# A fused transformer block on one core: attention's turns and values at other distances behind the logits, a compression layer cut in two jobs, later keys in other tiles

## The chip, the cores and the metric

The kernel runs on one core of a Trainium2 chip. The metric is the device time of the whole program in microseconds (us). Before the change it was 1020.26 us as the median of 3 runs (1019.53 to 1020.44). Differences of over about 0.2% (2 us) can be told from no change.

## The reference, cut to what matters

For 512 tokens of 1024 features the reference computes a half-weighted SwiGLU layer, a mixer, a second SwiGLU layer and a norm, in fp32:

```python
x = x + 0.5 * swiglu(rmsnorm(x, norm_ffn1), w_ffn1_gate, w_ffn1_up, w_ffn1_down)
x = x + hybrid_mixer(rmsnorm(x, norm_mix), ...)      # the change is in here
x = x + 0.5 * swiglu(rmsnorm(x, norm_ffn2), w_ffn2_gate, w_ffn2_up, w_ffn2_down)
return rmsnorm(x, norm_final)
```

The mixer projects the tokens to queries, keys and values for 16 heads of 64 features. Eight are MoBA heads (0 to 7): with 512 tokens and blocks of 256 their selection takes in all earlier blocks, so they come to causal attention with a bias by distance. Eight are NSA heads (8 to 15, in two groups of four): each is the gated sum of three attentions, over selected keys (`ks`), over a window (`kw`) and over 31 compressed keys (`cmp`). The compressed keys and values come out of a small two-layer network over blocks of 32 tokens, silu(blocks @ w1) @ w2, one for keys and one for values. All heads are put side by side and multiplied by `w_out`.

## The kernel before, in words

**Exact products.** TensorE multiplies in a reduced fp32 form, so an operand is split into a high and a low half (ScalarE copies, VectorE or GpSimd subtracts) and `mm3` (L86) makes three products: L87, L88, L89. Weights come in chunks of 128 x 1024 through three `raw` tiles; `halves` (L73) splits them (`whi` on ScalarE L81, `wlo` L82). While `side[0]` is set, from L1062 to the end of the mixer, `wlo` is made by GpSimd, otherwise by VectorE.

**Attention in steps.** A head, or a head and kind for NSA, is three steps of `chunks_of_head` (L878), over the four blocks of 128 queries: (0, 1), (2), (3). A step has three parts. *Logits* (L886): products L908 and L909 into a PSUM tile `ps_s`; VectorE adds the bias and takes the row's extreme (L916), ScalarE takes the exponential (L918, Exp), and where the step ends a row's work VectorE inverts the sum (L923) and GpSimd scales the row in place (L929) by it and by a gate. The rows lie in `lpn` tiles (four of them) and `lp` tiles (two). *Turn* (L931): TensorE transposes the scaled blocks (L938) into `ps_t`, ScalarE copies the high half to `th` (L941), VectorE makes the low half `tl` (L942). A head's first turn, of block column 0, needs the scaled rows of all four query blocks. *Values* (L947): products L93 and L94 of `th` and `tl` with the values into a PSUM tile `po`. After a head's last values `out_halves` (L850) splits the head's output into `oT`. Between NSA heads stand four steps of `cmp_pair` (L963): their logits go to `ps_c`, their turn writes a `th` tile of which there is one, shared with the 512-wide turns, and their values (L1006) read it. There are 76 steps, 52 of NSA and 24 of MoBA.

**The order on TensorE** is written out by hand (L1093 on). In round i the logits of step i are issued, then the turn of step i-4, then the values of step i-7; after each, `run` (L1034) issues other work, in units of three products (0.69 us), up to a target which a table `share` sets. The other work is a `stream` (L824) of jobs, each loading its weights two jobs ahead: `pre`, which is done before the first step, `fill` and `last` (L1021 to L1031). `proj` (L580) are the projections (eight units, PSUM `pp`), `w_out` (L805) is the output projection (PSUM `pw`), `khid` and `vhid` are the first layer of the compression for keys and values (PSUM `pc`), and `ksec` and `vsec` its second layer: `second` (L749) transposes the hidden values (L753, PSUM `pct`), splits them (L758, L759), loads and splits w2 (L761 to L765) and multiplies (PSUM `pck`) in one job. `need` (L1052) runs the stream until something is there. The order on the other engines is set by the tile scheduler, from the order of the program and its own estimate of when things are ready; tiles are given out of pools by it too. PSUM tags s, t, o and mm have two banks each; `pc`, `pct`, `pck`, `ps_t` share t, and `ps_c`, `pp`, `pw` share mm.

**Keys and queries** of MoBA: `moba_t` (L650) scales a projection; `stack_k` (L620) splits it and moves the halves by eight DMAs on SyncE's queue (L609) into four tiles, two of the high halves first; `stack_q` (L611) does so with four DMAs into two `aq` tiles. The keys of all four pairs go to `ak` tiles, six in all, which compression uses too. The keys of pairs 0 and 1 are stacked as soon as they are projected, those of pairs 2 and 3 by `moba_split` (L660), which `ahead` (L1040) calls when head 3 or 5 starts. NSA's values and keys lie in 12 `kvn` tiles, which the outputs `oT` of heads 0 to 7 take over.

## Time and profile before

One execution was profiled. Its span is from the first to the last instruction; its own time has some 2 us around that.

| | us |
|---|---|
| median of the runs | 1020.26 |
| the profiled execution | 1019.0 |
| its span | 1017.2 |
| TensorE busy in it | 982.8 |
| VectorE busy | 716.8 |
| ScalarE busy | 511.9 |
| GpSimd busy | 153.2 |

The attention stage runs from 424.7 us (the first logits) to 639 us (the last values). TensorE's idle time and its granted clock there are what to look for: a row of the waits names who waited, for whom, how long in all, how often and the longest. A row of the timeline has start, duration, engine, line, operation, tile written <- tiles read, and in brackets the idle time ahead of it with what ended it. PE is TensorE, DVE VectorE, ACT ScalarE, POOL GpSimd, SP SyncE.

### The profile page before, as it was taken

Reading aid. Unit: us, or ns where it says so; the run is one execution under the profiler, and the core shown is the slowest. Engines: PE = TensorE matmul, PEld = TensorE weight load, DVE = VectorE, ACT = ScalarE, POOL = GpSimd, SP = SyncE. Lnnn points to the kernel's source line nnn. Section 1 sums busy time; section 2 is a strip of 40 time slices with the busy share of each in tenths; the row PEclk is TensorE's granted clock in tenths of the full one; section 3 lists DMA queues with packets and bytes.
Section 4 is the critical chain, followed back from the end, with each engine's and each line's share of the span. In section 5 each row is a group of like instructions: output and inputs, shape, how many; then the busy total and the mean of one; then the engine's idle time right before and its main releaser. Section 6 shows DMA issues by size and latency. Waiting matters only on the chain. (4 is left out here: it accounts for less than half of the span.)

```text
span 1017.2 us, 15533 instructions
## 1 busy us (share of the span) xinstructions
PE 982.8 (97%) x5944; PEld 866.3 (85%) x5944; DVE 716.8 (70%) x1117; ACT 511.9 (50%) x871; POOL 153.2 (15%) x187
## 2 busy tenths in 40 slices
PE   9999999999999999879899997999999999999997
PEld 7889899999999898668778786888899999999995
DVE  5995686777774666557887766678957777767743
ACT  7553443444443554656766756545534444444444
POOL 0000000000000343235444542610000000000002
PEclk9999999999999999979999999999999999999999
DMA  9534265332301236721232522363332323432102
GB/s 331 215 103 132 76 209 146 125 108 80 116 34 39 78 108 200 223 67 52 61 81 73 153 84 55 110 232 107 101 125 92 116 79 109 125 113 92 45 1 83
DMA packets 45742, 113.86 MB, mean 112 GB/s; under 512 B 10049, under 2 KB 14866, under 8 KB 45668
## 3 DMA queue, kind: packets, MB, share of 16 engines
q1 hardware_dynamic: 45380, 112.73, 35.0%
q8 instruction: 47, 0.77, 0.3%
q14 instruction: 27, 0.22, 0.1%
q10 hardware_dynamic: 288, 0.14, 0.1%
HBM read 100.08 MB, written 5.30 MB: 104 GB/s over the span
## 5 line engine op out<-in xcount | busy, mean ns | idle before, releaser
L197 ACT ACTIVATE sph<-aw 128x1024 fp32r<-128x1024 f32 x114 | 121.0, 1061 | 238.5 <-PE pu L88 118.5
L198 DVE TENSOR_TENSOR spl<-aw,sph 128x1024 fp32r<-128x1024 f32 x114 | 139.3, 1222 | 37.0 <-ACT sph L197 36.9
L81 ACT ACTIVATE whi<-raw 128x1024 fp32r<-128x1024 f32 (+3 forms) x115 | 111.9, 976 | 103.9 <-PE pd L88 30.9
L88 PE MATMUL pd<-h,whi 128*128 128x512 f32 x320 | 126.4, 395 | 0.0
L87 PE MATMUL pd<-h,whi 128*128 128x512 f32 x320 | 126.1, 394 | 0.0
L89 PE MATMUL pd<-h,wlo 128*128 128x512 f32 x320 | 125.2, 391 | 0.0
L82 DVE TENSOR_TENSOR wlo<-raw,whi 128x1024 fp32r<-128x1024 f32 (+3 forms) x89 | 110.2, 1240 | 20.4 <-ACT whi L81 18.9
L89 PE MATMUL pu<-th,spl 128*128 128x256 f32 x384 | 106.9, 278 | 0.0
L87 PE MATMUL pu<-th,sph 128*128 128x256 f32 x384 | 106.9, 278 | 0.0
L88 PE MATMUL pu<-tl,sph 128*128 128x256 f32 x384 | 106.7, 278 | 0.0
L287 DVE TENSOR_TENSOR aw<-aw 128x1024 f32<-128x1024 f32 x64 | 78.0, 1220 | 29.1 <-DMA aw<-in_wgu 29.1
L469 DVE SCALAR_TENSOR_TENSOR x<-pd,x 128x512 f32<-128x512 f32 x72 | 49.3, 688 | 46.9 <-PE pd L89 46.9
L88 PEld LDWEIGHTS pu<-tl,sph 128*128 128x128 f32 x384 | 72.6, 189 | 3.9
L87 PEld LDWEIGHTS pu<-th,sph 128*128 128x128 f32 x384 | 72.1, 188 | 4.3
L87 PE MATMUL pgu<-xo,whi 128*128 128x512 f32 x192 | 75.1, 391 | 0.2 <-ACT xo L123 0.2
L88 PE MATMUL pgu<-xo,whi 128*128 128x512 f32 x192 | 74.8, 390 | 0.3 <-DVE xo L124 0.3
L89 PE MATMUL pgu<-xo,wlo 128*128 128x512 f32 x192 | 74.8, 389 | 0.0
L89 PEld LDWEIGHTS pu<-th,spl 128*128 128x128 f32 x384 | 72.1, 188 | 0.0
L89 PEld LDWEIGHTS pd<-h,wlo 128*128 128x128 f32 x320 | 60.1, 188 | 13.4
L89 PE MATMUL pw<-xo,spl 128*128 128x256 f32 x256 | 70.9, 277 | 0.0
L87 PE MATMUL pw<-xo,sph 128*128 128x256 f32 x256 | 70.8, 276 | 0.0
L88 PE MATMUL pw<-xo,sph 128*128 128x256 f32 x256 | 70.8, 276 | 0.0
(254 smaller groups left out, 2465.2 us busy)
## 6 DMA issues: line engine op xcount, KB each, us to landing
aw<-in_wgu SPq DMA_DIRECT2D x64, 512.0 KB, 4.0
raw<-in_wgu SPq DMA_DIRECT2D x23, 512.0 KB, 5.6
raw<-in_wd SPq DMA_DIRECT2D x22, 512.0 KB, 3.5
raw<-in_wd2a SPq DMA_DIRECT2D x18, 512.0 KB, 3.6
raw<-in_w_a SPq DMA_DIRECT2D x16, 512.0 KB, 3.5
raw<-in_w SPq DMA_DIRECT2D x8, 512.0 KB, 5.0
aq<-xo SPq DMA_DIRECT2D x32, 128.0 KB, 2.3
raw<-in_w_o SPq DMA_DIRECT2D x16, 256.0 KB, 2.7
```

The lines of the kernel that those rows point to most:

```text
L81: nc.scalar.activation(hi[:, s], src[:, s], AF.Copy)
L82: (nc.gpsimd if side[0] else nc.vector).tensor_tensor(lo[:, s], src[:, s], f32(hi[:, s]), ALU.subtract)
L87: nc.tensor.matmul(p, w[0], v[0], start=first, stop=False, skip_group_check=again)
L88: nc.tensor.matmul(p, w[0], v[1], start=False, stop=False, skip_group_check=again)
L89: nc.tensor.matmul(p, w[1], v[0], start=False, stop=last, skip_group_check=again)
L197: nc.scalar.activation(hi, v, AF.Copy)
L198: nc.vector.tensor_tensor(lo, v, f32(hi), ALU.subtract)
L287: nc.vector.tensor_tensor(to, x, y, op)
L469: nc.vector.scalar_tensor_tensor(xs[d], p, 0.5, xs[d], ALU.mult, ALU.add)
```

## The change

The turn of a step now stands six steps behind its logits (four before) and the values nine (seven before). In each round the values come first, then the turn, then the logits. The first six rounds get 1.5 units of other work more, the other shares are a little lower, and a fifth `lpn` tile is added. `second` is cut into two jobs, `turned` (transposes and their halves) and `second` (the products), with other jobs between; w2 is now loaded and split while the third chunk of the first layer is multiplied. In `pre`, `vhid`'s chunks stand ahead of the last chunk of `vm` (MoBA's values). Only the keys of pair 0 are stacked at once; those of pairs 1 and 3 go to `kvn` tiles, those of pairs 0 and 2 to `ak` tiles.

```diff
-                if kind == "k" and pair < 2:
+                if kind == "k" and not pair:
                     moba_k(pair)
...
-            got["k", pair] = stack_k(got["k", pair], [akt() for _ in range(4)])
+            got["k", pair] = stack_k(got["k", pair], [kvn() if pair % 2 else akt() for _ in range(4)])
...
-            if pair >= 2:
+            if pair:
                 moba_k(pair)
...
+                    if c == 8:
+                        second_weights()
...
-            def second(w):
+            def second_weights():
+                w2 = tmp.tile([128, 2, 64], F32, name="w2", tag="t", bufs=6)
+                nc.sync.dma_start(w2, A["w2"][which])
...
+            def turned(w):
                 hid = p[1]
                 pp = pt("t", "pct")
...
+            def second(w):
+                w2h, w2l, hh, hl = kept
                 pp = pt("t", "pck")
...
-            return proj(8 + which, blocks), [hidden(c) for c in range(0, 16, 4)], (None, second)
+            return proj(8 + which, blocks), [hidden(c) for c in range(0, 16, 4)], [(None, turned), (None, second)]
...
-                    lp = ap.tile([128, 384], F32, name="lpn", tag="lpn", bufs=4)
+                    lp = ap.tile([128, 384], F32, name="lpn", tag="lpn", bufs=5)
...
-               proj(11, nsa_k("kw")), khid[3], vm[2], ksec, vhid[0], proj(12, nsa_q(0)), vhid[1], vm[3], vhid[2], vhid[3],
-               (None, marked)]
-        fill = [proj(13, nsa_q(1)), vsec, proj(14, nsa_q(2)), proj(15, nsa_q(3))]
+               proj(11, nsa_k("kw")), khid[3], vm[2], ksec[0], vhid[0], vhid[1], proj(12, nsa_q(0)), ksec[1],
+               vhid[2], vhid[3], vm[3], (None, marked)]
+        fill = [proj(13, nsa_q(1)), vsec[0], proj(14, nsa_q(2)), vsec[1], proj(15, nsa_q(3))]
...
-        share = [0.65 if i < n_nsa else 0.6 for i in range(len(steps) + 7)]
+        share = [0.6 if i < n_nsa else 0.55 for i in range(len(steps) + 9)]
...
+            if i < 6:
+                share[i] += 1.5
...
-            for i in range(len(steps) + 7):
-                for j, lag in enumerate((0, 4, 7)):
+            for i in range(len(steps) + 9):
+                for n, (j, lag) in enumerate(((2, 9), (1, 6), (0, 0))):
                     if 0 <= i - lag < len(steps):
                         steps[i - lag][j]()
```

TensorE has 5748 rows of instructions before and after; only their order differs. Three places, each with TensorE's or ScalarE's rows (the changed kernel has other line numbers there: L919 and L920 are the logits, L949 the turn, L929 the exponential, L747 the Silu, L758 w2h).

TensorE before, ahead of the first turn (`ps_t`), at the end of the fifth logits (`ps_s`):

```order
L87 MATMUL pp<-xo,whi 128x512
L88 MATMUL pp<-xo,whi 128x512
L89 MATMUL pp<-xo,wlo 128x512
L908 MATMUL ps_s<-kvn,aq 128x384
L909 MATMUL ps_s<-kvn,aq 128x384
L938 MATMUL ps_t<-ident,lpn 128x128 x3
L938 MATMUL ps_t<-ident,lp 128x128
```

The same place now, at the end of the sixth logits:

```order
L87 MATMUL pp<-xo,whi 128x512
L88 MATMUL pp<-xo,whi 128x512
L89 MATMUL pp<-xo,wlo 128x512
L919 MATMUL ps_s<-kvn,aq 128x512
L920 MATMUL ps_s<-kvn,aq 128x512
L87 MATMUL pp<-xo,whi 128x512
L88 MATMUL pp<-xo,whi 128x512
L89 MATMUL pp<-xo,wlo 128x512
L949 MATMUL ps_t<-ident,lpn 128x128 x3
L949 MATMUL ps_t<-ident,lp 128x128
```

Between the first logits and the first turn stood five logits and 6 products of a projection; now there are six logits, 30 products and two small transposes.

ScalarE before, from the last chunk of `vm` to the first exponentials (`hid` is the hidden layer of the compressed values, L745 its Silu):

```order
L690 ACTIVATE vm<-pv,rc_94 128x8x64 x4
L81 ACTIVATE whi<-raw 128x1024 x2
L743 ACTIVATE hid<-pc 64x256
L81 ACTIVATE whi<-raw 128x1024
L918 ACT_TABLE_LOAD
L918 ACTIVATE lpn,m<-lpn,m 128x128
L918 ACTIVATE lpn,m<-lpn,m 128x256
L918 ACTIVATE lpn,m<-lpn,m 128x384
L745 ACT_TABLE_LOAD
L745 ACTIVATE hid<-hid 64x256
L918 ACT_TABLE_LOAD
L918 ACTIVATE lp,m<-lp,m 128x512
```

The same place now:

```order
L81 ACTIVATE whi<-raw 128x1024
L758 ACTIVATE w2h<-w_4117 128x128
L747 ACTIVATE hid<-hid 64x256
L690 ACTIVATE vm<-pv,rc_94 128x8x64 x4
L81 ACTIVATE whi<-raw 128x1024
L929 ACT_TABLE_LOAD
L929 ACTIVATE lpn,m<-lpn,m 128x128
L929 ACTIVATE lpn,m<-lpn,m 128x256
L929 ACTIVATE lpn,m<-lpn,m 128x384
L929 ACTIVATE lp,m<-lp,m 128x512
```

The Silu (now L747) stands ahead of `vm`, and one table load is left where there were three.

TensorE before, at the second layer for the values:

```order
L93 MATMUL po<-th,kvn 128x128
L94 MATMUL po<-tl,kvn 128x128
L753 MATMUL pct<-ident,hid 128x64 x2
L87 MATMUL pck<-w2h,hh 32x64
L88 MATMUL pck<-w2l,hh 32x64
L89 MATMUL pck<-w2h,hl 32x64
```

And now, at its transposes:

```order
L89 MATMUL pp<-xo,wlo 128x512
L766 MATMUL pct<-ident,hid 128x64 x2
L919 MATMUL ps_s<-kvn,aq 128x384
L920 MATMUL ps_s<-kvn,aq 128x384
L87 MATMUL pp<-xo,whi 128x512
```

The products into `pck` followed the transposes at once; now 47 rows stand between, some 10 us of TensorE's work.

## The prediction

> **What bounds the kernel now.** I read the page first, then the busy time by stage, then TensorE's waits by stage, then the timeline at the longest of them.

> ```profile
> span 1017.2 us, 15533 instructions
> PE 982.8 (97%) x5944; PEld 866.3 (85%) x5944; DVE 716.8 (70%) x1117; ACT 511.9 (50%) x871; POOL 153.2 (15%) x187
> ```

> TensorE (PE) is busy for 97% of the span, so it is the bound, and its work is the same after the change: 5748 rows in another order. What can be won is its idle time, 1017.2 - 982.8 = 34.4 us, and time in which it runs at a lower clock. The next view has engines by stretch; PEclk is the granted clock.

> ```profile
> core 0: us, PE busy (x) PEld busy (x) DVE busy (x) ACT busy (x) POOL busy (x), PEclk, DMA share, GB/s
> 434.00:441.00 7.00, 6.14 (x24) 5.10 (x24) 2.75 (x10) 4.43 (x15) 3.30 (x6) 0.57 0.11 30
> 451.00:457.00 6.00, 5.17 (x26) 4.66 (x27) 2.70 (x11) 1.76 (x6) 0.00 (x0) 0.50 0.61 176
> 460.00:600.00 140.00, 131.00 (x752) 110.42 (x751) 110.69 (x304) 96.18 (x243) 71.13 (x94) 1.00 0.31 84
> 613.00:618.00 5.00, 4.77 (x24) 4.33 (x24) 2.36 (x8) 3.19 (x9) 0.00 (x0) 0.66 0.45 118
> ```

> Two short stretches behind 434 and 451 us, and one behind 613, have a clock near half. Now TensorE's waits from 400 to 460 us (the second compression layers and the start of attention):

> ```profile
> PE ps_t L938 <- POOL lpn L929: 2.7, 3, 2.2
> PE pck L87 <- ACT w2h L764: 2.7, 2, 1.8
> PE ps_t L938 <- POOL lp L929: 2.4, 1, 2.4
> PE pck L88 <- DVE w2l L765: 2.0, 1, 2.0
> ```

> From 460 to 600 us (the rest of NSA and the first MoBA heads):

> ```profile
> PE ps_t L938 <- DVE tl L942: 3.6, 4, 1.5
> PE po L94 <- DVE tl L942: 1.3, 3, 0.5
> PE ps_s L909 <- DMA ak<-xo: 1.2, 1, 1.2
> PE po L93 <- ACT th L941: 1.0, 2, 0.5
> PE ps_t L938 <- DVE m L923: 0.8, 1, 0.8
> PE ps_s L908 <- DVE m L916: 0.6, 2, 0.3
> PE ps_t L938 <- POOL lp L929: 0.5, 2, 0.2
> ```

> From 600 to 660 us (the last MoBA heads):

> ```profile
> PE ps_s L909 <- DMA ak<-xo: 2.3, 1, 2.3
> PE ps_t L938 <- DVE tl L942: 1.4, 2, 0.9
> PE ps_t L938 <- POOL lp L929: 1.4, 2, 1.0
> PE ps_s L908 <- DMA ak<-xo: 1.3, 1, 1.3
> ```

> These sum to 9.8, 9.0 and 6.4: 25.2 of the 34.4 us of idle time are in the stage that the change reorders. So the question for each row is whether the new order puts work into it.

> **The first turn.**

> ```profile
> 424.69 0.22 PE L908 MATMUL ps_s<-kvn,aq 128*128 128x128 f32 x1
> 430.93 0.33 PE L938 MATMUL ps_t<-ident,lpn 128*128 128x128 f32 x1 [2.20 <-POOL lpn L929]
> 434.86 0.47 PE L938 MATMUL ps_t<-ident,lp 128*128 128x128 f32 x1 [2.43 <-POOL lp L929]
> 435.56 0.63 PE L88 MATMUL pp<-xo,whi 128*128 128x512 f32 x1
> 435.99 0.63 PE L89 MATMUL pp<-xo,wlo 128*128 128x512 f32 x1
> 445.28 0.39 PE L87 MATMUL pp<-xo,whi 128*128 128x512 f32 x1
> 445.51 0.39 PE L88 MATMUL pp<-xo,whi 128*128 128x512 f32 x1
> ```

> The turn's last block comes 434.86 - 424.69 = 10.2 us after the first logits. ScalarE has a detour within that:

> ```profile
> 429.91 1.28 ACT L745 ACT_TABLE_LOAD   x1
> 431.20 0.42 ACT L745 ACTIVATE hid<-hid 64x256 f32<-64x256 f32 x1
> 432.93 0.72 ACT L918 ACTIVATE lp<-lp,m 128x512 f32<-128x512 f32 x1
> ```

> A load, the Silu and a load back take 432.93 - 429.91 = 3.0 us. The new order does the Silu ahead of `vm`, so the chain is some 10.2 - 3.0 = 7.2 us. TensorE's side: products of 512 columns start every 445.51 - 445.28 = 0.23 us, so the 30 products that now stand ahead of the first turn are 6.9 us; six logits are some 2.4 us (the five of before took 424.69 to 428.7, less 6 products at 0.23 and 0.5 of waits, 2.1 us). The turn is due after 9.3 us, against a chain of 7.2. This wait, 2.7 + 2.4 = 5.1 us, goes. What is late next: behind the first turn the six steps issued ahead come due on VectorE and ScalarE together, with the halves of two projections among them. I trace the halves of the first turn and the rows of the fourth step to within a microsecond of their use, and leave 2.0 us of new waits: the term is **3.1** (0 to 5.1).

> **The second layers.** The rows of `pck` are 2.7 + 2.0 = 4.7 us, 0.9 of it in the keys' job and 3.8 in the values'. Now w2 is loaded and split under the first layer, and some 7 us (a projection and two `pc` chunks) and 10 us of other products lie between the transposes and `pck`. What stands in front of `hh` and `hl` on ScalarE and VectorE can't be ten times their 0.3 us. I leave 0.2: **4.5**.

> **The clock.** At full clock products start every 0.23 us, in the stretch behind the first turn every 435.99 - 435.56 = 0.43. The windows give a clock of 0.57 and 0.50: of the 6.1 us from 434.86 and the 5.2 us from 451.8, 0.43 and 0.50 are lost, 2.6 + 2.6 = **5.2**. Each stretch stands right behind two idle times of some 2 us, and the 140 us from 460 have the full clock, so it goes with those waits. [...]

> **NSA's other waits**, 460 to 600 us without the DMA's 1.2: 3.6 + 1.3 + 1.0 + 0.8 + 0.6 + 0.5 = 7.8 us. Rows that wait for the scaled rows (0.8 and 0.5) go: the distance from a head's last logits to its first turn was 2.9 to 6.3 us of TensorE's work in NSA and is now 5.2 to 8.7. The others:

> ```profile
> 470.64 0.50 PE L94 MATMUL po<-tl,kvn 128*128 128x512 f32 x1 [0.50 <-DVE tl L942]
> 501.12 0.52 PE L938 MATMUL ps_t<-ident,lpn 128*128 128x128 f32 x3 [1.37 <-DVE tl L942]
> ```

> The first stands behind the values of compression: the next 512-wide turn can only be copied when those have read the one `th` tile, and its values follow 1.5 us later in both orders. I halve it (1.3 + 1.0 gives 1.1), since the turn's copy now stands ahead of the exponentials on ScalarE. The second is a bank of `ps_t`: the `tl` that frees it is queued on VectorE behind a logits row that TensorE has not made yet. Turns follow each other as closely as before, but there are fewer such inversions in VectorE's order (7 for 11 over all steps), so I take half of 3.6, 1.8. The 0.6 stays. Sum: 1.3 + 1.1 + 1.8 = **4.2** (0 to 7.8).

> Against it stands what the change makes shorter: the values now follow their turn by 3.4 to 8.3 us of TensorE's work in NSA, where it was 4.8 to 8.3. The copy and its low half need some 0.6 + 0.7 us, more when exponentials stand ahead. No row of before shows this wait apart from the places above. If one in four of 48 turns is late by 0.25 us, that is **-3.0** (0 to -10).

> **The keys.** Pair 2's wait (1.2, at head 4) goes: the `ak` tiles hold only two pairs now, and on SyncE its eight DMAs stand a head earlier: **1.2**. Pair 3's (2.3 + 1.3) stays nearly:

> ```profile
> 607.67 4.95 SPq L609 DMA_DIRECT2D ak<-xo  x8
> 610.60 0.30 PE L908 MATMUL ps_s<-ak,aq 128*128 128x128 f32 x1 [1.28 <-DMA ak<-xo]
> 613.23 0.30 PE L909 MATMUL ps_s<-ak,aq 128*128 128x128 f32 x1 [2.33 <-DMA ak<-xo]
> ```

> Its keys are projected at the last moment in both orders, and what it waits for is eight issues of 0.62 us in a row, not a tile. The logits of head 6 now stand 3.7 us behind the projection instead of 3.1: **0.4** (counting the jitter of one DMA). The clock behind 613 us stays low.

> **The last heads and the end.** There the steps have no other work between them. The waits for `lp` (1.4) go with the longer distance, those for `tl` (1.4) stay: **1.4** (0 to 2.8). At the end one wait is new:

> ```profile
> 639.15 0.28 PE L94 MATMUL po<-tl,vm 128*128 128x128 f32 x1
> 642.01 1.26 DVE L867 TENSOR_TENSOR kvn<-to,u 64x512 fp32r<-64x512 f32 x1 [0.41 <-ACT u L866]
> ```

> From the last values to the output's low half are 643.27 - 639.15 = 4.1 us. Eight units (5.5 us) covered them; five units (3.4 us) are left, since the values come two rounds later: **-0.5**.

> **The sum**: 3.1 + 4.5 + 5.2 + 4.2 - 3.0 + 1.2 + 0.4 + 1.4 - 0.5 = 16.5 us. Against the profiled execution, 1019.0 (span 1017.2): 1002.5. The median of the runs shown is 1.3 above it, so the median to expect is 1020.3 - 16.5 = 1003.8 us.

> **Rivals.** (1) *The start stays a chain.* On ScalarE a split of weights (`whi`) whose load is issued late stands ahead of the first exponential; if that load lands some 3 us late, the first turn is late again and the clock falls behind it. Then 3.1 and one 2.6 are gone: a gain of 10.8, 1009.5 us. For it: the rows of `whi` are where ScalarE can be held; against it: the chain has 2.1 us to spare. (2) *The clock stays low where it was*, because it comes of something else than the waits: without 5.2 the gain is 11.3, 1009.0 us. [...] Against it: the full clock from 460 to 600 us, with shorter waits in the same kind of work. (3) *Slower: the halves of the turns become the bound.* VectorE is busy for 110.7 of 140 us from 460 to 600, ScalarE for 96.2, both in strict order; the values stand up to some 3 us closer to their turn, 2.5 us behind it in the last heads. If each of the 72 turns' halves comes late to its values, the loss reaches the other terms' 19.5 us at 0.27 us a turn; at 0.35 it is 25 us, and the time 1020.3 - 19.5 + 25 = 1026 us. For it: waits for `tl` and `th` are the most of NSA's. Against it: they stand at a shared tile and a bank, not at the ordinary turns. (4) *The keys' new tiles are not free in time*, since `kvn` tiles are freed only by the last values of NSA's first group: the waits of head 2 or 6 grow to some 4 us more; a gain of 12, 1008 us. Against it: the DMAs of pair 1 stand on SyncE's queue two heads ahead of their use.

> **How the numbers follow.** The forecast holds for gains from 13 to 24 us: 0.63. Rival 1 has 0.16, rival 2 0.07, rival 4 0.05. Rival 3 has 0.05, and 0.04 is a milder form of it, 0.20 to 0.27 us a turn: gains of 5 to 0 us, half of them under 2. Differences of over 0.2% (2.0 us) can be told from no change; so faster by more has 0.93, no change 0.02, slower 0.05. The range: its low end takes the terms of the start, of NSA and of the last heads near their upper bounds, 16.5 + 1 + 3 + 2 = 22.5 and a little, 997 us; its high end takes in rivals 1, 2 and 4, 1011.5 us.

> **What would show it.** Right: no wait of over 1 us for L929's rows ahead of the first turn; one table load between `vm` and the first exponentials; no wait at `pck`; a granted clock of 1.00 from 424 to 460 us; one DMA wait left, at head 6, of 3 to 3.6 us. Wrong: a wait of 2 us or more ahead of any of the first six turns, or waits at `po` that sum to over 6 us. A TensorE idle time of under 15 us in all would mean that I gave the values too much.

## The result, and the profile after

The changed kernel took 1006.98 us as the median of 4 runs (1002.16 to 1008.83), the kernel before 1020.17 on the same chip (1019.53 to 1020.44): a ratio of 0.9858, 95% interval 0.9827 to 0.9888, 13.2 us faster. The forecast was 1003.8 in a range from 997 to 1011.5. The profiled execution was the fastest of the four, 1002.16 us with a span of 1000.4: against the profiled execution of before (1019.0) it is 16.8 us faster, where the working came to 16.5.

The page of the changed kernel, its first lines:

```profile
span 1000.4 us, 15514 instructions
PE 974.6 (97%) x5944; PEld 860.0 (86%) x5944; DVE 719.5 (72%) x1117; ACT 509.4 (51%) x869; POOL 154.9 (15%) x187
```

TensorE's idle time fell from 34.4 to 1000.4 - 974.6 = 25.8 us, by 8.6. The other 8.2 us are busy time, 982.8 to 974.6, for the same 5944 instructions. Most of that is the clock: in the profile of before, three stretches at half clock (433.18 to 440.01, 450.24 to 457.07 and 614.08 to 617.49 us) hold 5.15, 5.24 and 3.41 us of busy time at a granted clock of 0.50, so by an estimate half of it, 6.9 us, is lost. Where the other 1.3 us lie is open. The busy time by stretch, with the same columns as before:

```profile
424.00:434.00 10.00, 8.66 (x43) 6.88 (x42) 7.78 (x21) 7.85 (x17) 5.95 (x7) 1.00 0.58 195
434.00:441.00 7.00, 7.00 (x41) 5.91 (x40) 5.37 (x19) 5.68 (x18) 5.00 (x6) 1.00 0.56 134
451.00:457.00 6.00, 6.00 (x40) 5.27 (x39) 4.20 (x16) 3.80 (x11) 3.57 (x7) 1.00 0.47 143
460.00:600.00 140.00, 127.37 (x728) 106.68 (x727) 111.33 (x298) 94.71 (x237) 70.05 (x93) 1.00 0.35 90
```

The clock is 1.00 in the two stretches that had 0.57 and 0.50, and the trace has no low stretch ahead of the end of the program. At the start, TensorE's first logits and first turn:

```profile
425.95 0.33 PE L919 MATMUL ps_s<-kvn,aq 128*128 128x128 f32 x1 [1.34 <-DVE vm L691]
435.92 0.49 PE L949 MATMUL ps_t<-ident,lpn 128*128 128x128 f32 x3
436.25 0.27 PE L949 MATMUL ps_t<-ident,lp 128*128 128x128 f32 x1
```

The turn waits for nothing. TensorE's waits from 400 to 460 us:

```profile
PE ps_s L919 <- DVE vm L691: 1.3, 1, 1.3
PE ps_t L949 <- DVE vc L799: 0.6, 1, 0.6
```

From 460 to 600 us:

```profile
PE ps_t L949 <- DVE tl L953: 4.7, 7, 1.1
PE ps_s L920 <- DMA kvn<-xo: 2.5, 1, 2.5
PE pw L88 <- DVE o L878: 1.7, 1, 1.7
PE ps_t L949 <- DVE m L934: 1.7, 1, 1.7
PE pw L87 <- ACT o L874: 0.7, 1, 0.7
PE po L94 <- DVE tl L953: 0.5, 1, 0.5
PE ps_t L949 <- DVE mc L997: 0.3, 1, 0.3
PE ps_s L919 <- DMA kvn<-xo: 0.2, 1, 0.2
PE ps_s L919 <- DVE m L927: 0.2, 1, 0.2
```

From 600 to 660 us one row is left:

```profile
PE ps_t L949 <- DVE tl L953: 2.3, 3, 1.0
```

The waits at `pck` and those for the scaled rows of the start are gone. New are the first logits' wait for `vm` (the last block of MoBA's values has to leave a PSUM bank first) and the output projection's for `o`, 2.4 us. The turns' waits for `tl` grew: 7.0 us in all, where they were 5.1.

### The profile page after: what moved, and what is told of

Read it like the earlier page. It is cut to its first block, busy times and chain, and to the rows that moved or that the text cites. A ratio compares the mean times of both kernels' runs of the same rounds, so it can differ in the third digit from the quotient of the medians.

```text
span 1000.4 us, 15514 instructions
## 1 busy us (share of the span) xinstructions
PE 974.6 (97%) x5944; PEld 860.0 (86%) x5944; DVE 719.5 (72%) x1117; ACT 509.4 (51%) x869; POOL 154.9 (15%) x187
## 4 chain that ended last, share of the span: by engine, by line
PE 89%; DVE 5%; DMA 2%; ACT 2%; issue 1%; POOL 1%; SPq 1%; DVEq 0%; ACTq 0%
PE pd L87 8%; PE pd L88 8%; PE pd L89 8%; PE pu L89 6%; PE pu L87 6%; PE pu L88 6%; PE pgu L88 4%; PE pgu L89 4%; PE pgu L87 4%; PE pw L87 4%; PE pw L88 4%; PE pw L89 4%; PE pp L87 2%; PE pp L89 2%; PE pp L88 2%; PE ps_t L949 2%
## 5 line engine op out<-in xcount | busy, mean ns | idle before, releaser
L88 PE MATMUL pd<-h,whi 128*128 128x512 f32 x320 | 126.3, 395 | 0.0
L87 PE MATMUL pd<-h,whi 128*128 128x512 f32 x320 | 126.1, 394 | 0.0
L89 PE MATMUL pd<-h,wlo 128*128 128x512 f32 x320 | 125.2, 391 | 0.0
L87 PE MATMUL pu<-th,sph 128*128 128x256 f32 x384 | 106.9, 278 | 0.0
L89 PE MATMUL pu<-th,spl 128*128 128x256 f32 x384 | 106.9, 278 | 0.0
L88 PE MATMUL pu<-tl,sph 128*128 128x256 f32 x384 | 106.7, 278 | 0.0
L88 PEld LDWEIGHTS pu<-tl,sph 128*128 128x128 f32 x384 | 72.6, 189 | 4.0
L87 PEld LDWEIGHTS pu<-th,sph 128*128 128x128 f32 x384 | 72.1, 188 | 4.3
L87 PE MATMUL pgu<-xo,whi 128*128 128x512 f32 x192 | 75.1, 391 | 0.2 <-ACT xo L123 0.2
L88 PE MATMUL pgu<-xo,whi 128*128 128x512 f32 x192 | 74.9, 390 | 0.3 <-DVE xo L124 0.3
L89 PE MATMUL pgu<-xo,wlo 128*128 128x512 f32 x192 | 74.8, 389 | 0.0
L89 PEld LDWEIGHTS pu<-th,spl 128*128 128x128 f32 x384 | 72.1, 188 | 0.0
L89 PEld LDWEIGHTS pd<-h,wlo 128*128 128x128 f32 x320 | 60.1, 188 | 13.4
L89 PE MATMUL pw<-xo,spl 128*128 128x256 f32 x256 | 70.9, 277 | 0.0
L87 PE MATMUL pw<-xo,sph 128*128 128x256 f32 x256 | 70.8, 276 | 0.0
L88 PE MATMUL pw<-xo,sph 128*128 128x256 f32 x256 | 70.8, 276 | 0.0
```

The source lines that it names most:

```text
L87: nc.tensor.matmul(p, w[0], v[0], start=first, stop=False, skip_group_check=again)
L88: nc.tensor.matmul(p, w[0], v[1], start=False, stop=False, skip_group_check=again)
L89: nc.tensor.matmul(p, w[1], v[0], start=False, stop=last, skip_group_check=again)
```

## The experiments

| kernel | median, us | runs | ratio to the kernel before, same chip (95%) |
|---|---|---|---|
| changed kernel, once more | 1005.1 | 1003.3 to 1005.9 | 0.9851 (0.9837 to 0.9865) |
| compression's part alone | 1015.5 | 1013.8 to 1016.3 | 0.9956 (0.9944 to 0.9969) |
| new distances alone | 1011.9 | 1011.3 to 1013.3 | 0.9923 (0.9911 to 0.9935) |
| keys' part alone | 1019.7 | 1018.3 to 1022.7 | 0.9998 (0.9987 to 1.0009) |
| changed, compression's part undone | 1014.0 | 1013.7 to 1017.3 | 0.9939 (0.9924 to 0.9955) |
| changed, no extra units at the start | 1008.3 | 1005.4 to 1009.7 | 0.9873 (0.9855 to 0.9892) |
| changed, Silu behind `vm` | 1006.9 | 1005.2 to 1008.4 | 0.9862 (0.9845 to 0.9880) |
| changed, two idle times shortened | 1000.5 | 999.8 to 1002.0 | 0.9801 (0.9786 to 0.9816) |
| that, turn behind logits | 1001.9 | 1000.4 to 1005.3 | 0.9818 (0.9799 to 0.9838) |
| that, first logits two units later | 1001.4 | 999.5 to 1007.7 | 0.9820 (0.9796 to 0.9844) |
| that, six short gaps added | 1012.0 | 1010.3 to 1016.6 | 0.9907 (0.9887 to 0.9927) |
| that, six longer gaps added | 1027.8 | 1024.8 to 1030.9 | 1.0067 (1.0044 to 1.0090) |

My theory was that of the prediction: the halved clock comes of the waits, and goes with them. The rivals are that the clock is low for another reason, and, for the sizes, that one of the three parts does nearly all.

### Which part does it

Compression's part alone: the kernel before with these lines of the change, `second` cut in two, and the new order of `pre` (the Silu ahead of `vm`).

```diff
+                    if c == 8:
+                        second_weights()
...
-        fill = [proj(13, nsa_q(1)), vsec, proj(14, nsa_q(2)), proj(15, nsa_q(3))]
+        fill = [proj(13, nsa_q(1)), vsec[0], proj(14, nsa_q(2)), vsec[1], proj(15, nsa_q(3))]
```

> The kernel before with the compression's part of the change alone (second layer in two jobs, w2 early, the order of the first jobs with the Silu ahead of vm). Theory A (the prediction): the waits at pck go (4.5), the clock behind them is full (2.6), and the first turn's chain loses the table loads and the Silu (3.0 of its 5.1 us of waits), after which the first stretch has its clock too (2.6): a gain of 10.1 to 12.7 us, some 1008 to 1010 us. Rival (the clock falls for another reason than these waits): 4.5 + 3.0 = 7.5 us, with the clock at 0.5 to 0.6 in both stretches. Rival (nearly all of the gain comes from the other distances): 2 us or less.

It gained 1019.8 - 1015.5 = 4.3 us: far less than theory A and the first rival gave, and more than the second rival. Its longest waits from 400 to 470 us, then three stretches:

```profile
PE po L1017 <- DMA vc<-vc: 2.8, 2, 2.3
PE ps_s L919 <- DVE vm L691: 1.7, 1, 1.7
PE ps_t L949 <- POOL lp L940: 0.7, 2, 0.4
PE pck L87 <- DVE tl L953: 0.5, 1, 0.5
```

```profile
424.00:431.00 7.00, 5.28 (x21) 4.18 (x21) 6.29 (x19) 6.43 (x16) 4.29 (x5) 0.76 0.62 214
457.50:461.00 3.50, 1.76 (x17) 0.87 (x15) 2.29 (x6) 2.78 (x8) 2.23 (x3) 1.00 0.00 0
461.00:468.00 7.00, 5.29 (x14) 3.75 (x15) 4.85 (x9) 3.09 (x6) 2.08 (x4) 0.51 0.49 113
```

The waits at `pck` and the first turn's nearly went, as worked out, but with the products in a later job `vc` and its copies by DMA are late for values that stand only seven steps behind. That wait is 2.8 us, and a clock of 0.51 for 7 us follows it. The 0.76 in the first stretch comes of 3.4 us at half clock from 427.0, in the window behind that of the new wait for `vm` (1.7 us). The low clock moved with the waits.

The new distances alone: the kernel before with the loop, the shares and the fifth `lpn` tile.

```diff
-                for j, lag in enumerate((0, 4, 7)):
+                for n, (j, lag) in enumerate(((2, 9), (1, 6), (0, 0))):
```

> The kernel before with the new distances alone (turns six and values nine steps behind, values first, the shares, the fifth lpn tile). The second layer is in one job, as before. Theory A: first turn 3.1 and its clock 2.6, NSA's waits 4.2 less 3.0, last heads 1.4, end -0.5: a gain of 7.8 us, with the waits at pck (4.7 us) and the low clock behind them (2.6) still there: some 1012 us. Rival (the distances move the waits only): a gain under 3 us. Rival (the clock is low for another reason than the waits): 5.2 us, with the clock near 0.57 behind the first turn though no wait of 2 us stands there.

It gained 7.9 us against an expected 7.8. That the two agree so closely is partly luck: its profile also has waits for `o` (2.4 us) and stretches at half clock from 568 and 606 us on that the working did not have, and 2.3 us less of waits for keys. The waits at `pck` stay, and so does the clock behind them:

```profile
PE pck L87 <- ACT w2h L764: 3.4, 2, 2.6
PE pck L88 <- DVE w2l L765: 0.9, 1, 0.9
```

```profile
434.00:438.00 4.00, 0.77 (x13) 0.66 (x14) 2.54 (x6) 2.23 (x8) 3.03 (x3) 1.00 0.32 77
438.00:442.00 4.00, 4.00 (x13) 3.20 (x13) 1.14 (x4) 1.16 (x4) 1.62 (x4) 0.57 0.74 203
```

The keys' part alone (with `if pair >= 2` turned into `if pair` as well).

```diff
-                if kind == "k" and pair < 2:
+                if kind == "k" and not pair:
...
-            got["k", pair] = stack_k(got["k", pair], [akt() for _ in range(4)])
+            got["k", pair] = stack_k(got["k", pair], [kvn() if pair % 2 else akt() for _ in range(4)])
```

> The kernel before with the keys' part alone (keys of pairs 1 and 3 in kvn tiles, those of pair 1 stacked later). Theory A: the wait at head 4 (1.2) goes, pair 3's (3.6) stays within 0.5, and the clock behind it (0.66 from 613 to 618 us, 1.6 us lost) stays: a gain of 1.0 to 1.6 us. Rival (tiles not free in time): the wait of head 2 or 6 grows, slower by up to 4 us. Rival (the clock's third stretch comes of the two waits of 1.3 and 2.3 together): 3 us, with a clock of 1.00 from 613 us.

No gain, where theory A gave 1.0 to 1.6: 0.1 us, within the interval. The wait at head 4 is still there at 1.1 us, and pair 3's are unchanged (1.3 and 2.3).

The changed kernel with compression's part undone (the first experiment's lines reversed).

> The changed kernel with the compression's part undone (second layer in one job, w2 loaded in it, the first jobs in the old order); distances and keys as changed. Theory A (the second layer is worth 4.5 us of waits and 1.7 to 3.4 us of clock whichever distances are used): 6 to 8 us slower than the changed kernel, 1011 to 1013. Rival (most of its gain was that of the old distances: alone it gave 4.3 us): 2 to 4 us slower, 1007 to 1009.

It stands 7.1 us under the kernel before, the changed kernel 14.7 in its own comparison: in place, compression's part is worth 7.6 us, where alone it gave 4.3. The parts alone sum to 12.3 us. The rest is an interplay, as far as it is clear of the noise (the first comparison gave 13.2 us, not 14.7): nine steps between logits and values, with the extra units of the first rounds, are what hides the later `vc`. In the changed kernel one wait of 0.6 us for it is left.

### The clock

> The changed kernel once more, word for word: its four first times lay between 1002.2 and 1008.8 us, where those of the kernel before lay within 1 us. Theory R1: the difference is the granted clock. In some executions it is halved for some microseconds behind the idle times that are left (0.7 + 1.7 us of the output projection at 558 to 560 us, 2.5 us of the keys' DMA at 598 us); then a longer execution has the same idle time of TensorE (25.8 us, within 1) and a stretch of 3 to 6 us at a clock near 0.5 behind one of them. Theory R2: the difference is in transfers that land late; then the clock is 1.00 and the idle time is longer by the difference. Expected: 1002 to 1009 us again.

The kernel is the same. The profiles of the two executions differ by 1.1 us of span: 0.7 us of idle time less stands against 1.8 us of busy time more. Both have the same wait for the keys, 2.46 us here, in the changed kernel's first profile:

```profile
596.57:599.98 3.41, 1.63 (x12) 1.63 (x13) 2.29 (x6) 1.87 (x6) 1.52 (x3) 1.00 0.85 196
599.98:603.39 3.41, 2.92 (x21) 2.38 (x20) 3.11 (x10) 3.31 (x9) 0.90 (x3) 1.00 0.18 63
```

and 2.44 us in the second one:

```profile
597.10:600.51 3.41, 1.39 (x10) 1.39 (x11) 2.16 (x6) 1.91 (x5) 1.78 (x4) 1.00 0.84 198
600.51:603.92 3.41, 3.41 (x15) 2.92 (x14) 3.10 (x11) 3.31 (x9) 0.65 (x2) 0.51 0.23 79
```

Every low stretch in the traces that ends before the kernel's end is 3.41 or 6.83 us long, and they lie on one grid of 3.41 us, so I cut the time into these windows. The first profile has 1.63 us of work in the window of the wait, the second 1.39, since the grid lies a little differently in it; only there is the next window at half clock. (I cut the windows to within some 0.1 us of the clock's steps; the reading is the same with exact ones, 1.65 and 1.44.) R1 holds for this pair. It is not shown for the longer executions, of 1005 to 1009 us, of which none was profiled: the mean granted clock fits the slowest (0.992 against 0.998 is some 6 of the 6.7 us between them), but one of 1006.6 us had 0.997, which is worth about 1 of its 4.4. In the profile of before, the start of attention:

```profile
429.77:433.18 3.41, 0.98 (x3) 0.41 (x3) 0.63 (x3) 3.35 (x6) 2.28 (x4) 1.00 0.65 227
433.18:440.01 6.83, 5.15 (x16) 4.20 (x17) 2.63 (x10) 4.39 (x15) 2.70 (x5) 0.50 0.15 45
```

Over all 14 profiles, from 380 to 690 us and with the windows set on the clock's own steps, a window that itself has the full clock is followed by one at half clock in 21 of 21 cases where TensorE was busy for under 1.5 us, in 7 of 25 from 1.5 to 1.95, and in none of 1178 above. The next two kernels test this with gaps of a chosen length, in the kernel with the two idle times shortened (below): every fifth unit of what `stream` has left behind the last step gets these lines, the shorter gaps with `range(1)`.

```diff
+                p = pt("t", "gap")
+                nc.tensor.transpose(p[:, :128], ident, ident)
+                g = tmp.tile([128, S], F32, name="gap", tag="t", bufs=6)
+                nc.scalar.activation(g[:, :128], p[:, :128], AF.Copy)
+                for _ in range(5):
+                    nc.scalar.activation(g[:, :128], g[:, :128], AF.Copy)
+                p = pt("t", "gap")
+                nc.tensor.transpose(p[:, :128], g[:, :128], ident)
```

> The kernel of c1_gaps with idle times put into the dense products of the output projection behind attention: six times, with 15 products (3.4 us) between, a small transpose, a chain of two small copies on ScalarE and a transpose of their result stand in TensorE's order, so TensorE waits for the chain, some 1.0 to 1.4 us each time. Theory G (a window of 3.41 us with TensorE busy for less than about half of it is followed by one at half clock): no window has less than 2 us of work, so the clock stays full there; only the idle times are added, 6 to 9 us, some 1007 to 1010. Rival (any wait of over 1 us can cost clock): low stretches behind some of the six, 1.7 us each.

> As g_short, but with six copies in each chain, some 2.2 to 2.8 us of idle time each of six times; the fifth has four products' triples in its middle, so it may be covered. Theory G: where 1.75 us or more of a gap fall into one window, the next is at half clock; by the place of the gap in the window that happens to some two of three gaps of 2.4 us. The profile shows 2 to 5 low windows behind the gaps and the time is 5 to 6 times 2.4 us longer for the idle times and 3 to 9 us longer for the clock: 1016 to 1023 us. [...]

In both kernels the fifth chain is covered and five of the six show as waits. ScalarE did not always take a chain up at once (in the longer kernel the first copy of the first chain starts 0.7 us behind the start of its transpose, that of the last 1.0), and the gaps are longer than meant, and less even: 0.9 to 2.35 us, 7.2 in all, and 2.45 to 3.72, 15.8 in all. The longer ones, TensorE's rows at their ends:

```profile
632.74 0.33 PE L1129 MATMUL gap<-ident,gap 128*128 128x128 f32 x1 [3.44 <-ACT gap L1127]
639.93 0.33 PE L1129 MATMUL gap<-ident,gap 128*128 128x128 f32 x1 [3.30 <-ACT gap L1127]
648.28 0.48 PE L1129 MATMUL gap<-ident,gap 128*128 128x128 f32 x1 [2.88 <-ACT gap L1127]
656.13 0.33 PE L1129 MATMUL gap<-ident,gap 128*128 128x128 f32 x1 [2.45 <-ACT gap L1127]
```

and the same kernel by windows:

```profile
627.65:631.06 3.41, 1.65 (x8) 1.08 (x6) 0.86 (x3) 1.96 (x5) 1.27 (x1) 1.00 0.07 26
631.06:634.47 3.41, 1.74 (x8) 1.47 (x9) 1.33 (x2) 2.16 (x6) 0.14 (x1) 1.00 0.27 77
637.89:641.30 3.41, 1.37 (x7) 1.16 (x8) 0.92 (x1) 1.89 (x6) 2.05 (x2) 1.00 0.42 120
641.30:644.71 3.41, 3.41 (x10) 2.62 (x9) 0.32 (x1) 0.63 (x1) 0.00 (x0) 0.51 0.08 34
644.71:648.13 3.42, 0.69 (x4) 0.29 (x2) 1.12 (x2) 2.86 (x8) 2.55 (x2) 0.99 0.30 84
648.13:651.54 3.41, 3.26 (x8) 2.59 (x9) 0.00 (x0) 0.09 (x1) 0.00 (x0) 0.51 0.18 70
```

The longest of these four, 3.44 us, is split by a window's edge (1.65 and 1.74 us of work) and costs nothing. The gap of 3.30 leaves 1.37 us in its window and that of 2.88 leaves 0.69; both are followed by half clock, and the last gap of that kernel, 3.72 us, by two such windows. So is the short kernel's gap of 2.35 us (1.06 us of work left) by one, while its others cost none; its two other low windows stand at the first logits and at the keys' wait. The length of a wait decides little; the work left in a window does. Theory G holds for where the low windows are. Both times came out above what it gave, only in part because the gaps were longer than planned; what the added instructions cost besides was not worked out.

The two idle times shortened:

```diff
-                    while 2 * k + 1 not in out_done:
+                    while rnd[0] < out_done.get(2 * k + 1, 1000) + 2:
...
-            for n, part in enumerate(halves_of_rows(t)):
-                for i in range(2):
+            parts = halves_of_rows(t)
+            for n, i in ((0, 0), (1, 0), (0, 1), (1, 1)) if by_head else ((0, 0), (0, 1), (1, 0), (1, 1)):
```

(`out_done` now holds the round, and `by_head` is set for pair 3.)

> The changed kernel with two of its new idle times taken away: the output projection's products of an NSA head are issued two rounds after that head's last values, not in the same round (its waits of 0.7 and 1.7 us at 558 to 560 us), and the keys of pair 3 are moved in the order in which the two heads need them (its wait of 2.5 us at 598 us, two issues of 0.62 us less). Theory G: the granted clock is decided in windows of 3.41 us, the length of the low stretches; a window in which TensorE is busy for less than about half (1.4 to 1.9 us) is followed by one at half clock, which costs 1.7 us, and where the windows lie differs from one execution to the next. By it 2.4 and 1.2 us of waits go, some 0.5 to 1 us of it comes back as waits of turns that have less other work, and the low windows behind these two places go or become rarer: 1000 to 1003 us against 1005 for the changed kernel, with less spread (3 us or less). Rival (the waits only): 2 to 3 us less than the changed kernel, the spread as before. Rival (the waits come back at the turns): within 1 us of the changed kernel.

The lowest median of this study, 1000.5 us, and its five runs lie within 2.2 us. Of its waits from 540 to 600 us these are left of the two places:

```profile
PE pw L88 <- DVE o L878: 1.2, 1, 1.2
PE ps_s L919 <- DMA kvn<-xo: 0.9, 1, 0.9
PE ps_s L920 <- DMA kvn<-xo: 0.4, 1, 0.4
```

They are 2.5 us where they were 5.1, but TensorE's idle time as a whole is only 1.0 us less (its span of 999.5 less 974.7 busy gives 24.8). Yet the ratio is 0.9801 against 0.9851: some 5 us. Its runs have mean granted clocks of 0.998 to 0.999, those of the changed kernel 0.992 (the slowest, 1008.8 us) to 0.998 (the fastest, 1002.2), 0.995 to 0.996 in the mean. By an estimate from these means some 3 of the 5 us are clock; the rest is not placed. No window of its attention stage is at half clock in its profile; the least work in one is 1.66 us, which the counts above put among those that can go either way.

### The start

> The changed kernel without the 1.5 units of other work more in each of the first six rounds; the nine units (27 products) come later. Theory A (the prediction's working of the first turn: a chain of 7.2 us on VectorE, ScalarE and GpSimd against 9.3 us of TensorE's work): only some 3 products of 30 and six logits (2.4 us) stay ahead of the first turn, so it waits for its scaled rows by 3 to 5 us, and the clock falls behind that (1.7 or 3.4 us more): 1009 to 1012 us, less what the nine units cover later (up to 2 us). Rival (the distance of six steps alone hides the first turn): no change within 1 us of the changed kernel, 1005 us.

```diff
-            if i < 6:
-                share[i] += 1.5
```

By the medians it is 1.3 to 3.2 us slower than the changed kernel, by the ratios 1.5 to 2.2, and the intervals overlap, so the time alone decides little. Its profile does show a loss, but not at the first turn. I had also miscounted what stays ahead of that (three units, not one). Its rows there, and its longest wait from 400 to 470 us:

```profile
425.76 0.33 PE L919 MATMUL ps_s<-kvn,aq 128*128 128x128 f32 x1 [1.83 <-DVE vm L691]
432.19 0.33 PE L949 MATMUL ps_t<-ident,lp 128*128 128x128 f32 x1 [0.42 <-POOL lp L940]
```

```profile
PE po L1017 <- DMA vc<-vc: 3.9, 2, 3.4
```

The chain is 432.19 - 425.76 = 6.4 us (7.2 in the prediction), and 0.4 of it shows as a wait. What the nine units are needed for is `vsec`: without them `vc` is late by 3.4 us in spite of the nine steps, and one window at half clock follows.

```diff
-               vhid[2], vhid[3], vm[3], (None, marked)]
+               vhid[2], vm[3], vhid[3], (None, marked)]
```

> The changed kernel with the last two jobs ahead of attention exchanged: vm's last chunk, then the last chunk of the first layer, whose Silu so comes between the first exponentials again, with a table load on either side. Theory A: the wait of the first logits for vm's evacuation (1.3 us, which the prediction missed) goes, since a job lies between; the chain of the first turn gets its 3.0 us back (7.2 to 10.2) against 9.3 us of work, so a wait of 1 to 2 us comes there: no change within 1.5 us, 1004 to 1006. Rival (the first turn is no longer bound by that chain): the 1.3 us are won, 1003 to 1004. Rival (the chain of ScalarE is tighter than worked out): waits of 3 us or more at the first turn and a low clock behind, 1008 or more.

No difference to the changed kernel that can be told. The wait for `vm` goes, but the chain's 3.0 us come back at another place than I said, the bank of the fifth step's logits, which VectorE frees only behind the reciprocal of the first rows:

```profile
435.68 0.69 PE L919 MATMUL ps_s<-kvn,aq 128*128 128x384 f32 x1 [2.60 <-DVE m L927]
```

Two windows at half clock (435.0 to 441.8 us) begin within it. ScalarE's queue at the start does matter, as the prediction had it.

The first logits two units later, in the kernel with the shortened idle times:

```diff
+            run(3)
             for i in range(len(steps) + 9):
```

> The kernel of c1_gaps with the first logits two units (6 products, 1.4 us) later: three units of a projection stand ahead of them where one stood. Theory (the first logits wait for a PSUM bank until VectorE has taken vm's last block out of it, 1.3 to 2.3 us in the profiles, and the first turn has work to spare: its scaled rows came 6.4 us after the first logits even where only a third of the work stood in between): that wait falls to 0 to 0.9 us, no new one at the first turn, 998.5 to 1000 us. Rival (the first turn needs those units): a wait of about 1.4 us comes there, no change within 0.7 us, 1000.5. The low clock that follows this wait in one profile in twelve would go as well.

The wait for `vm` is gone from the profile and idle time is 1.4 us less (999.2 - 975.8 = 23.4). (Low clock behind that wait stands in two profiles, not in one: compression's part alone and the shorter gaps.) The time is the same within the intervals: the profiled run has a window at half clock behind 595 us, and one run of six took 1007.7. Whether the 1.4 us would show without that stays open.

### The waits for the turns' low halves

```diff
-                for n, (j, lag) in enumerate(((2, 9), (1, 6), (0, 0))):
+                for n, (j, lag) in enumerate(((2, 9), (0, 0), (1, 6))):
```

> The kernel of c1_gaps with the turn behind the logits in each round (values, logits, turn) where it was values, turn, logits. The waits of turns for the low half of an earlier turn (6.4 us in nine places) are the largest that are left; VectorE takes the logits' rows and the low halves in the order of the program. Theory T (the low half stands on VectorE behind a row of logits that TensorE has not made yet): with the logits ahead of the turn this wait falls by half or more, 2 to 4 us, 997 to 999 us. Rival (the two banks of the turns are simply too few, and VectorE too busy): the same waits within 1.5 us, the time within 1.5 us of 1000.5. Rival (the logits' own bank becomes late): slower by 2 us or more.

The turns' waits for `tl` fall from 6.4 to 2.1 us, as the theory of VectorE's order has it, but the values' waits for it grow from 0.5 to 3.5, and the time is the same within the intervals. In its profile TensorE idles for 1.3 us less (23.5 against 24.8), but the waits for pair 3's keys are 2.9 us where they were 1.3, and with a window at half clock (0.52) behind them TensorE's busy time is 1.9 us longer. Both rows of `tl`:

```profile
PE po L94 <- DVE tl L953: 3.5, 4, 1.0
PE ps_t L949 <- DVE tl L953: 2.1, 4, 0.6
```

## Why the prediction was right, and where not

The time came out within the range, 3.2 us above the forecast. That the profiled pair gave 16.8 us beside a sum of 16.5 is luck: two errors cancel in it. Idle time fell by 8.6 us where the terms without the clock gave 11.3, and busy time by 8.2 where the clock's term was 5.2. Point by point:

- **First turn**, 3.1: 5.1 us of waits went and 1.9 came (`vm` 1.3, `vc` 0.6), so 3.2. The size and the lone table load are right. The 2.0 of new waits stand at other places than those named, and most of the 30 products that I had cover the chain are not needed for it: with 9 of them the wait is 0.4 us. The others make `vc` early enough.
- **Second layers**, 4.5: 4.7, no wait at `pck` is left. What the step overlooked is that the values' products come later with it; the nine steps and the extra units together pay for that.
- **Clock**, 5.2: 6.9 of the 8.2 us of busy time, by the low stretches of before. The two stretches of the term gave their 5.2. That the low clock goes with the waits is shown, by the parts alone and by the gaps. The mis-sized part is the third stretch, "the clock behind 613 us stays low", worth 1.7: its window had 1.63 us of work left after the change, in this execution. In the second profile of the same program it stays low. How long a gap is does not settle it: one of 2.35 us cost a window, one of 3.44 us none.
- **NSA's other waits**, 4.2, less 3.0 for the shorter way to the values: the 7.8 us are now 9.8 (the rows from 460 to 600 us without the DMA's). Three things failed. Half of the waits for `tl` were to go, by a count of inversions; they grew from 3.6 to 4.7, and why is open: the experiment on the order of turn and logits moves most of them to the values. A wait for `m` of 1.7 came, which the last section takes up. And I did not look at who else reads `o`: with the values first in a round, the output projection follows them at once and waits 2.4 us. The -3.0 was mis-sized the other way: waits of values fell from 2.3 to 0.5 us, so what rival 3 feared did not come.
- **Keys**, 1.6: 4.8 us of DMA waits are 2.7, so 2.1. But the tiles are not the reason: alone they gained nothing and head 4's wait stayed, while the new distances alone brought the 4.8 down to 2.5. The 0.4 was an estimate with the jitter of a DMA in it, which no run shows: the two profiles of the changed kernel have this wait at 2.46 and 2.44 us.
- **Last heads**, 1.4: 2.8 us are 2.3, so 0.5. **End**, -0.5: no such wait in the profile.

The median gained less than the profiled pair, 13.2 and 14.7 us for 16.8. The changed kernel's profiled execution was its fastest and has no low window in the attention stage; by their mean clocks (0.992 to 0.997) most of the others have some.

## What to carry to other kernels

Judge TensorE's waits by what they leave in a window of the clock, not one by one: here a wait of 2.35 us was followed by a window at half clock, one of 3.44 us that a window's edge cut in two was not, and a kernel with two waits shortened by 2.6 us was 5 us faster. A kernel whose runs spread by several us may have windows near the bound found here, 1.5 to 1.95 us of work in 3.41; look there first. Before a part of a change is called good or useless, look for what the other parts hide for it.

## What the runs showed of the hardware

VectorE's additions end late here where GpSimd is at work. In the changed kernel one addition of `out_halves` (`to` and `u` into the low half) takes 2.83 us; the median of its kind is 0.92 or less. VectorE's rows, then GpSimd's:

```profile
493.79 2.83 DVE L878 TENSOR_TENSOR o<-to,u 64x512 fp32r<-64x512 f32 x1
498.30 0.14 DVE L934 RECIPROCAL m<-m 128x1 f32<-128x1 f32 x1
```

```profile
493.67 2.40 POOL L82 TENSOR_TENSOR wlo<-raw,whi 128x1024 fp32r<-128x1024 f32 x1
```

It starts just behind GpSimd's split of a weight chunk and ends 0.55 us behind that one's end, and the turn that needs `m` waits for 1.7 us. The second profile has the same 2.83 us, so it is set by the order and not by chance. Nor is it one place: the 14 profiles have 224 of these additions. Leaving GpSimd's memsets aside, 71 began with no GpSimd operation under way and took 0.65 to 0.72 us. Of the 153 that began while GpSimd was splitting or scaling, 146 ended 0.53 to 0.63 us behind the end of that operation, however long it still had to run (up to 2.35 us); the other 7 began within 0.02 us of GpSimd's start and took 0.69 to 0.73. That this place costs the 1.7 us is likely but not isolated: in the kernel without the extra units the split comes later, the addition takes 0.94 us and the wait for `m` is not there, but other rows have moved too.
